# Adding expert results to the output rows in DRAM by indirect writes that add

## The chip, the cores and the metric

The kernel runs on one core of a Trainium2 chip. The metric is the device time of one execution in microseconds. A core has a matmul engine (TensorE, PE in the profile, with PEld for its weight loads), a vector engine (VectorE, DVE), an activation engine (ScalarE, ACT), a general engine (GpSimd, POOL) and a queue engine that only issues transfers here (SyncE, SP). All transfers run on 16 DMA engines. SP issues the plain ones; POOL issues the indirect ones, in which a list of row numbers in on-chip memory says which rows of a DRAM tensor are read or written, and a row number out of bounds skips its row.

## The reference, cut to what matters

The program computes two transformer blocks on 512 tokens of 1024 channels. The change touches the last stage only, the mixture of experts, which adds to each token's row the results of two experts out of 32. The two experts of a token always lie in the same group of eight.

```python
N_GROUPS = 4
EXPERTS_PER_GROUP = 8
EXPERT_FF = 256
TOP_K_EXPERTS = 2
...
    for g in range(N_GROUPS):
        a = jnp.einsum('nd,edf->nef', hf, w_gate[g])
        b = jnp.einsum('nd,edf->nef', hf, w_up[g])
        hid = jax.nn.silu(a) * b * gates[:, g, :, None].astype(hf.dtype)
        out = out + jnp.einsum('nef,efd->nd', hid, w_down[g])
    return out.reshape(B, S, D)
...
        h = rmsnorm(x, ffn_norm[l])
        x = x + hierarchical_moe(h, router_group_w[l], router_group_b[l], router_expert_w[l],
                                 router_expert_b[l], expert_w_gate[l], expert_w_up[l],
                                 expert_w_down[l])
```

`gates` is zero for the experts that a token did not choose, so the kernel computes only the chosen ones.

## The kernel before, in words

Everything up to about 1060 us is the first block, and the attention and memory attention of the second. Its last step, `cross_out` (line 1160), finishes the residual rows in an on-chip tile `fx` (4 tiles of 128 tokens by 1024 channels, 2 MB) and writes them to a DRAM tensor `x3d` (line 1175), from which the expert stage gathers rows.

**The expert stage** has 16 rounds of two experts, `2r` and `2r + 1` (line 1489). Each expert has 64 places of the 128 of a round. A list made on chip gives each place its token or none (`lists_of`, `places`); the 1024 results of 512 tokens fill about half of the 2048 places. A round:

- waits for its weights: per expert one gate and one up matrix of 1 MB each (`load_gu`, L1023 or L1026) and a down matrix of 1 MB (`load_dn`, L1039 or L1045), all issued by SP. Their buffers come from four pools of slots: `a16` has six slots of 2 MB, `w16` two, `e8` three of 1 MB, `wr` two of half a MB. `PLACES` (line 1054) says which pool the matrices of a round take, in a pattern of three rounds. In `a16`, `fx` holds one slot to the end of the program (allocated at line 1135), so five are left for gate and up matrices. The first four experts' are fetched at line 1056, the fifth's at line 1137.
- gathers its token rows from `x3d` with one indirect transfer of POOL (`fetch_rows`, L1343) into one of three tiles `hg`, three rounds ahead. Round 0 has its rows from matmuls instead (`rows_of`, L1302).
- transposes them (`turn_rows`, L1352), multiplies by gate and up (`expert_up`, L1368, `pgu`), applies the activation and the gate (L1372, L1373), transposes (L1383) and multiplies by the down matrices (`expert_down`, `pdn`).
- puts its result away in one of two manners. **Rows of a table** (10 rounds, L1392 to L1398): the two halves are copied to an on-chip tile `yr` and one indirect transfer of POOL writes its rows to a DRAM table `yd` of 1024 rows, at the token's number for its first expert and 512 further for its second. **One-hot put-back** (rounds 2, 5, 8, 11, 14 and 15, `ONEHOT` at line 1488, L1401 to L1452): the result is split into two tiles of a reduced type, a one-hot matrix is made from the token list (L1416), and 16 matmuls (L1427) with 8 additions (L1428) put the rows into `fx`. The put-back of one round is done in the next; that of round 14 is added up with that of round 15 in the same matmuls.

In the last round `results` (line 1456) reads both halves of `yd` back (L1463, 8 transfers of 512 KB), POOL adds the halves (L1464), DVE adds the sum to `fx` (L1466), and `fx` is written to `out` (L1445). `yd` is filled with zeros far earlier (line 515), in the first block.

The order of the instructions on each engine and queue is set by a scheduler that goes by its own estimate of times. It puts in the waits: an instruction waits for what it reads to be written, and a slot or a DRAM tensor is only written again when earlier uses are over.

Of the kernel before, what the change touches and what calls it, by code (L numbers as in the profile page):

```python
# [15 lines left out]
S = 512  # L16
D = 1024
# [44 lines left out]
def program(tc, I, out, sb, ps, dr, dbg, upto):  # L62
# [6 lines left out]
    def c1(shape, name, dt=F32):  # L69
        return sb.tile(shape, dt, name=name)  # L70
# [7 lines left out]
    def s4(name, shape=(128, 2, 512), dt=F32):  # L78
        return sb.tile(list(shape), dt, name=name, tag="s4", bufs=8)
# [432 lines left out]
    yd = dr.tile([2 * S, D], F32, name="yd")  # L512
    zero = s4("zero", (128, D))
    nc.gpsimd.memset(zero, 0.0)
    nc.scalar.dma_start(yd.rearrange("(i p) d -> p i d", p=128), ap_of(zero, 0, [[0, 8], [1, D]]))


# [19 lines left out]
    tk = c1([128, 8], "tk")  # L537
    nc.vector.tensor_scalar(tk[:, 0:4], ctok, -NOTOK, None, OP.add)
    nc.vector.tensor_scalar(tk[:, 4:8], ctok, S - NOTOK, None, OP.add)
# [516 lines left out]
    gus = [load_gu(e, str(e)) for e in range(4)]  # L1056
# [78 lines left out]
    fx = a16("fx", F32, (128, 4, D))  # L1135
    nc.sync.dma_start(fx, x2d.rearrange("(i p) d -> p i d", p=128))
    gus.append(load_gu(4, "4"))
# [22 lines left out]
    def cross_out(i):  # L1160
# [14 lines left out]
        nc.sync.dma_start(x3d[i * 128:(i + 1) * 128, :], xt)  # L1175

# [25 lines left out]
    def route(i):  # L1202
# [19 lines left out]
        def gates():  # L1222
# [14 lines left out]
            for j in range(2):  # L1237
                V_.tensor_scalar(R0[:, j, i, :], ohs[:, j, i, :], tk[:, 4 * j + i:4 * j + i + 1], None, OP.mult)
# [11 lines left out]
    def count(i):  # L1250

        for i2 in range(i + 1):
            nc.tensor.matmul(cnts[:, i * 32:(i + 1) * 32], trib if i2 == i else oneb, mh[:, i2, :],
                             start=i2 == 0, stop=i2 == i)
        vv = carve(2)
        V_.scalar_tensor_tensor(vv, cnts[:, i * 32:i * 32 + 2], 1.0, mh[:, i, 0:2], OP.add, OP.mult)
        V_.tensor_tensor(sel[:, i], ap_of(iota, 1, [[0, 2], [1, 64]]), ap_of(vv, 0, [[1, 2], [0, 64]]), OP.is_equal)
# [8 lines left out]
    def lists_of(p, i, src):  # L1266


        for j in range(2):
            for par in range(2):  # L1270
                nc.tensor.matmul(p[64 * par:64 * par + 64, 0:16], am[:, i, j, :],
                                 ap_of(src[:, j, i, :], par, [[2, 16]]),
                                 start=j == 0 and i == 0, stop=j == 1 and i == 3)
# [45 lines left out]
    def tokens(p, n, name):  # L1319

        src = sb.tile([128, n], I32, name=name + "_i", tag=name[:2] + "_i")
        V_.tensor_scalar(src, p, NOTOK, None, OP.add)
        e = sb.tile([128, n], F32, name=name + "_e", tag=name[:2] + "_e")
        V_.tensor_scalar(e, p, NOTOK, None, OP.add)
        return src, e

    def places(p, n):

        row, rowf = c1([128, n], "row", I32), c1([128, n], "rowf")
        V_.tensor_scalar(row, p, NOTOK, None, OP.add)  # L1330
        V_.tensor_scalar(rowf, p, NOTOK, None, OP.add)
        src, e = c1([128, n], "srci", I32), c1([128, n], "srcf")
        V_.tensor_scalar(e, rowf, float(S), -float(S), OP.is_ge, OP.mult)
        V_.tensor_tensor(e, e, rowf, OP.add)
        V_.tensor_copy(src, e)
        return row, src, e

    hg = [s4(f"hg{b}", (128, D)) for b in range(3)]
    for b in range(3):
        nc.gpsimd.memset(hg[b], 0.0)  # L1340
# [35 lines left out]
    def expert_down(sh, ws, src, name, last=False, row=None, hold=False, held=None):  # L1376

# [7 lines left out]
        if row is not None:  # L1385
            yr = s4(f"yr{name}", (128, D))
            for half in range(2):
                hs = slice(half * 512, half * 512 + 512)
                po = psm(f"pdn{name}_{half}")
                for f in range(2):  # L1390
                    for a, (gu, dn) in enumerate(ws):
                        nc.tensor.matmul(po[m * a:m * a + m, :], hd[:, f, m * a:m * a + m], dn[f][:, hs],  # L1392
                                         start=f == 0, stop=f == 1)
                if half:
                    V_.tensor_copy(yr[:, hs], po)
                else:
                    nc.scalar.activation(yr[:, hs], po, AF.Copy)
            nc.gpsimd.indirect_dma_start(out=yd, out_offset=bass.IndirectOffsetOnAxis(ap=row, axis=0), in_=yr,  # L1398
                                         in_offset=None, bounds_check=2 * S - 1, oob_is_err=False)
            return None  # L1400
        yh, yl = s4(f"yh{name}", (128, D), F32R), s4(f"yl{name}", (128, D), F32R)  # L1401
        put = []

        def down(half):
# [6 lines left out]
            split(po, yh[:, hs], yl[:, hs])  # L1411

        def where():
            put.append(w2(f"put{name}", dt=F32R))
            for i in range(4):
                V_.tensor_scalar(put[0][:, i * 128:(i + 1) * 128], iota, float(128 * i), src, OP.add, OP.is_equal)  # L1416

        def terms(i, half):
            hs = slice(half * 512, half * 512 + 512)
            return [(put[0][:, i * 128:(i + 1) * 128], t[:, hs]) for t in (yh, yl)]  # L1420

        def add(i, half):
            p = (pmm if half else psm)(f"pad{name}_{i}_{half}")
            hs = slice(half * 512, half * 512 + 512)
            ts = (held(i, half) if held else []) + terms(i, half)
            for x, (a, b) in enumerate(ts):
                nc.tensor.matmul(p, a, b, start=x == 0, stop=x == len(ts) - 1)  # L1427
            V_.tensor_tensor(fx[:, i, hs], fx[:, i, hs], p, OP.add)  # L1428

        def add_rows():  # L1430
            where()
            for i in range(4):
                for half in range(2):
                    add(i, half)

        if last:
            where()
            for half in range(2):
                down(half)
            results()  # L1440
            for half in range(2):
                hs = slice(half * 512, half * 512 + 512)
                for i in range(4):
                    add(i, half)
                    nc.sync.dma_start(out[0, i * 128:(i + 1) * 128, hs], fx[:, i, hs])  # L1445
            return None
        for half in range(2):
            down(half)
        if hold:
            where()  # L1450
            return terms
        return add_rows  # L1452

    row, srci, srcf = places(plist[:, 0:16], 16)

    def results():

        ys = [sb.tile([128, 4, D], F32, name=f"yt{j}", tag=tag, bufs=n)
              for j, (tag, n) in enumerate((("w16", 2), ("a16", 6)))]
        for i in range(4):  # L1460
            for j in range(2):
                t = ys[j][:, i, :]
                nc.sync.dma_start(t, yd[j * S + i * 128:j * S + (i + 1) * 128, :])  # L1463
            nc.gpsimd.tensor_tensor(ys[0][:, i, :], ys[0][:, i, :], ys[1][:, i, :], OP.add)  # L1464
        for i in range(4):
            V_.tensor_tensor(fx[:, i, :], fx[:, i, :], ys[0][:, i, :], OP.add)  # L1466

    for r in range(1, 4):
        fetch_rows(hg[r % 3], srci[:, r:r + 1])
# [17 lines left out]
    add_rows = None  # L1487
    ONEHOT = (2, 5, 8, 11, 14, 15)
    for r in range(16):
        es, (gtags, dtags), last = (2 * r, 2 * r + 1), PLACES[r % 3], r == 15  # L1490
        gu, fetch = [], []
        for e, tag in zip(es, gtags):
            if e < len(gus):
                gu.append(gus[e])
            else:
                t, f = load_gu(e, str(e), tag, True)
                gu.append(t)
                fetch += f
# [8 lines left out]
        rows = turn_rows(hg[r % 3], f"{r}") if r else rows0  # L1507
        sh = expert_up(rows, grs[:, 1, r:r + 1], grs[:, 0, r:r + 1], ws, f"{r}",
                       None if r else other_lists)
        if r and r + 3 < 16:  # L1510
            fetch_rows(hg[r % 3], srci[:, r + 3:r + 4])
        if add_rows and not last:
            add_rows()
        add_rows = expert_down(sh, ws, srcf[:, r:r + 1], f"{r}", last, None if r in ONEHOT else row[:, r:r + 1],
                               r == 14, add_rows if last else None)
# [6 lines left out]
    with tc.If(nval > CAP):  # L1522
        with tc.For_i(0, 32, 1) as e:
# [6 lines left out]
            for j in range(2):  # L1530
# [4 lines left out]
                V_.scalar_tensor_tensor(rx[:, :, 0], rx[:, :, 2], 0.0, tk[:, 0:4], OP.is_gt, OP.mult)  # L1535
                Rx.append(rx)
            for rr in range(4):
# [7 lines left out]
                si, sf = tokens(p[:, 0:1], 1, f"lx{rr}")  # L1545
                gx_ = sb.tile([128, 2], F32, name=f"lx{rr}_g", tag="lx_g")
                V_.tensor_copy(gx_, p[:, 1:3])
                fetch_rows(hg[rr % 3], si)
                sh = expert_up(turn_rows(hg[rr % 3], f"x{rr}"), gx_[:, 1:2], gx_[:, 0:1], ws, f"x{rr}")
                expert_down(sh, ws, sf, f"x{rr}")()  # L1550
        for i in range(4):
            nc.sync.dma_start(out[0, i * 128:(i + 1) * 128, :], fx[:, i, :])
# [21 lines left out]
```

## Time and profile before

| | |
|---|---|
| median of 3 runs | 1313.07 us (1309.04 to 1313.3) |
| the profiled execution, its own time | 1309.88 us |
| its span, from first to last instruction | 1308.1 us |
| PE busy in the span | 1263.4 us, 97% |
| DVE, ACT, POOL busy | 711.3, 490.3, 234.0 us |
| moved by the DMA engines | 218.62 MB, of which indirect 6.50 MB |
| expert stage, from the first `pgu` matmul to the end | 1059.0 to 1308.1 us |

Times in the rows are microseconds from the start of the span unless a row says ns. PE's matmuls are pipelined, and their ends are modelled, so that a busy PE is not a PE at its peak. A DMA share of 1 means that the 16 DMA engines are busy all the time. "To landing" is the time from the issue of a transfer to its completion. The idle time of an engine is put down to what released it last.

### The profile page before, as it was taken

The page shows a single profiled execution, that of the slowest core. Times are in us where ns is not written, and L with a number is a line of the kernel's source. Part 1 is how long each engine was busy: PE and PEld are TensorE (multiplying, and loading weights), DVE is VectorE, ACT ScalarE, POOL GpSimd, SP SyncE. Part 2 cuts the span into 40 slices and gives each one's busy share as a digit, 9 for nine tenths or more (in the row PEclk, how much of TensorE's full clock was granted, in tenths as well). Part 3 has the DMA queues.
Part 4 walks back from the last instruction along what each step waited for, and adds up shares of the span by engine and source line. Part 5 has one row for each costly group of instructions (what it writes and reads, how often), then busy time and mean ns, then how long its engine had stood idle before and what let it go on. Part 6 is the DMA issues. An engine that isn't in the chain of part 4 may idle for free.

```text
span 1308.1 us, 20715 instructions
## 1 busy us (share of the span) xinstructions
PE 1263.4 (97%) x8406; PEld 1000.3 (76%) x8406; DVE 711.3 (54%) x1299; ACT 490.3 (37%) x859; POOL 234.0 (18%) x278
## 2 busy tenths in 40 slices
PE   6999999999999999999999999999999999999986
PEld 5898989889988888888899977967897853343433
DVE  4567676676573244543556579993346643233225
ACT  4456454546432244422434333456435311101100
POOL 2203012030110000000001455553011120110103
PEclk9999999999999999999999999999999999999998
DMA  6321222222363243233653312224178479999995
GB/s 191 97 83 53 92 66 66 83 70 75 113 258 95 67 128 94 71 94 98 207 172 106 100 49 73 65 69 146 65 243 336 162 266 416 419 418 418 419 414 226
DMA packets 118085, 218.62 MB, mean 167 GB/s; under 512 B 15280, under 2 KB 94896, under 8 KB 106849
## 3 DMA queue, kind: packets, MB, share of 16 engines
q1 hardware_dynamic: 107248, 202.08, 42.9%
q10 hardware_dynamic: 7136, 8.67, 2.0%
q0 software_dynamic: 3600, 6.50, 1.3%
q8 instruction: 68, 1.11, 0.4%
q14 instruction: 33, 0.26, 0.1%
HBM read 206.00 MB, written 17.83 MB: 171 GB/s over the span
## 4 chain that ended last, share of the span: by engine, by line
PE 83%; DVE 6%; DMA 6%; ACT 2%; issue 1%; POOL 1%; ACTq 0%; DVEq 0%; POOLq 0%
PE pgu L1368 8%; PE pl L327 2%; PE pf L162 2%; PE pwo L161 2%; PE pf L163 2%; PE pdn L1392 2%; PE pwo L162 2%; PE pf L161 2%; PE pwo L163 2%; DMA gu<-in_expert_w_gate 2%; PE pdn L1409 1%; PE pq L163 1%; PE ps L780 1%; DMA gu<-in_expert_w_up 1%; PE pq L161 1%; PE pq L162 1%
## 5 line engine op out<-in xcount | busy, mean ns | idle before, releaser
L1368 PE MATMUL pgu<-gu,hgT 128*64 128x512 f32 x512 | 119.0, 595 | 3.7 <-DMA gu<-in_expert_w_up 2.2
L1368 PEld LDWEIGHTS pgu<-gu,hgT 128*64 128x64 f32 x512 | 39.8, 137 | 71.7 <-issue 66.4
L361 ACT ACTIVATE qk<-G 128x512 f32<-128x512 f32 x112 | 69.1, 665 | 51.6 <-DVE G L351 51.6
L1373 DVE SCALAR_TENSOR_TENSOR sh<-sh,grs,pgu 128x256 f32<-128x256 f32 x16 | 7.7, 480 | 105.4 <-ACT sh L1372 105.4
L1372 ACT ACTIVATE sh<-pgu,grs 128x256 f32<-128x256 f32 x16 | 7.6, 474 | 139.2 <-PE pgu L1368 139.2
L348 DVE TENSOR_TENSOR G<-G,T 128x512 f32<-128x512 f32 x56 | 39.2, 701 | 31.4 <-ACT qk L361 28.6
L312 POOL TENSOR_TENSOR T<-T 128x512 f32<-128x512 f32 (+6 forms) x56 | 37.0, 660 | 42.6 <-DVE T L279 38.8
L1343 POOL DMA_INDIRECT hg<-x3d,srci x15 | 15.4, 1025 | 157.5 <-PE thg L1352 109.4
L161 PE MATMUL pi<-wi,hT_h 128*128 128x256 f32 x128 | 37.8, 296 | 3.3 <-ACT wi L139 1.8
L351 DVE TENSOR_TENSOR G<-G,T 128x512 f32<-128x512 f32 x56 | 38.8, 694 | 0.0
L162 PE MATMUL pi<-wi,hT_h 128*128 128x256 f32 x128 | 37.7, 294 | 0.0
L1392 PE MATMUL pdn<-dn,sh 128*64 128x512 f32 x160 | 37.4, 601 | 0.1
L163 PE MATMUL pi<-wi,hT_l 128*128 128x256 f32 x128 | 37.3, 291 | 0.0
L161 PE MATMUL pv<-wv,hT_h 128*128 128x256 f32 x128 | 36.8, 288 | 0.0
L163 PE MATMUL pv<-wv,hT_l 128*128 128x256 f32 x128 | 36.7, 286 | 0.0
L162 PE MATMUL pv<-wv,hT_h 128*128 128x256 f32 x128 | 36.5, 286 | 0.0
L162 PE MATMUL pg<-wga,hT_h 128*128 128x256 f32 x128 | 36.5, 285 | 0.0
L161 PE MATMUL pg<-wga,hT_h 128*128 128x256 f32 x128 | 36.4, 285 | 0.0
L163 PE MATMUL pg<-wga,hT_l 128*128 128x256 f32 x128 | 36.2, 283 | 0.0
L132 POOL TENSOR_SCALAR nm_r<-nm_q 128x1 f32<-128x1 f32 x2 | 2.5, 1254 | 182.5 <-ACT nm_s L200 182.4
L327 PE MATMUL pl<-qk 128*64 128x64 f32 x896 | 34.3, 225 | 0.0
L327 PEld LDWEIGHTS pl<-qk 128*64 128x64 f32 x896 | 29.3, 137 | 6.2 <-issue 2.1
(554 smaller groups left out, 4080.9 us busy)
## 6 DMA issues: line engine op xcount, KB each, us to landing
gu<-in_expert_w_gate SPq DMA_DIRECT2D x32, 1024.0 KB, 19.3
gu<-in_expert_w_up SPq DMA_DIRECT2D x32, 1024.0 KB, 18.4
dn<-in_expert_w_down SPq DMA_DIRECT2D x27, 1024.0 KB, 20.0
wo_r<-in_w_out SPq DMA_DIRECT2D x16, 512.0 KB, 3.6
wq_r<-in_w_in SPq DMA_DIRECT2D x12, 512.0 KB, 4.3
dn<-in_expert_w_down SPq DMA_DIRECT2D x10, 512.0 KB, 18.1
wi_r<-in_w_in SPq DMA_DIRECT2D x8, 512.0 KB, 6.5
wfb_r<-in_w_in SPq DMA_DIRECT2D x8, 512.0 KB, 4.3
```

The source lines that it names most:

```text
L161: nc.tensor.matmul(o, ah, bh, start=first, stop=False)
L162: nc.tensor.matmul(o, ah, bl, start=False, stop=False)
L163: nc.tensor.matmul(o, al, bh, start=False, stop=last)
L312: nc.gpsimd.tensor_tensor(ap_of(T, o, [[n2, 2], [1, n2]]), ap_of(T, a, [[sa, 2], [2, n2]]), ap_of(T, a + 1, [[sa, 2], [2, n2]]), OP.mult)
L327: nc.tensor.matmul(p[64 * j:64 * j + 64, c * 64:c * 64 + 64], kt[:, k0:k0 + 64], qt[:, q0:q0 + 64], start=True, stop=True)
L348: nc.vector.tensor_tensor(ap_of(G, 0, [[512, 2], [2 * m, nb], [1, m]]), ap_of(G, 0, [[512, 2], [2 * m, nb], [1, m]]), ap_of(T, a + 1, [[sa ...
L351: nc.vector.tensor_tensor(ap_of(G, 1024 + m, [[512, 2], [2 * m, nb], [1, m]]), ap_of(G, 1024 + m, [[512, 2], [2 * m, nb], [1, m]]), ap_of( ...
L361: nc.scalar.activation(ap_of(qk, a * 512, [[2 * m, nb], [m, 2], [1, m]]), ap_of(G, a * 512, [[2 * m, nb], [1024 + m, 2], [1, m]]), AF.Copy)
L780: nc.tensor.matmul(p[:, :n], qiT[hs, h // 2, i * 128:(i + 1) * 128], kiT[hs, :n], start=True, stop=True)
L1343: nc.gpsimd.indirect_dma_start(out=h, out_offset=None, in_=x3d, in_offset=bass.IndirectOffsetOnAxis(ap=sidx, axis=0), bounds_check=S - 1, ...
L1368: nc.tensor.matmul(pg[m * a:m * a + m, :], hT_[:, k, m * a:m * a + m], ap_of(gu, k * 256, [[2048, 2], [1, 256]]), start=k == 0, stop=k == 7)
L1392: nc.tensor.matmul(po[m * a:m * a + m, :], hd[:, f, m * a:m * a + m], dn[f][:, hs], start=f == 0, stop=f == 1)
```

## The change

`yd`, its zeros and the one-hot put-back go. `cross_out` writes each finished tile of residual rows to `out` as well as to `x3d`. Every round's result rows are copied to an on-chip tile and added to the rows of `out` by one indirect write of POOL that adds (`compute_op=OP.add`). [...] There are four tiles `hg` instead of three, and a round's result takes the tile from which its own token rows came, so the gather for round `r + 4` follows the write of round `r` on POOL and in the tile. `fx` is allocated ahead of the weights and has its last use before the expert rounds. The lists hold token numbers alone, without the offset of 512 for second experts. The loop for lists of more than 64 tokens (line 1522 on, not entered in the profiled execution) is changed to match.

```diff
-    yd = dr.tile([2 * S, D], F32, name="yd")
-    zero = s4("zero", (128, D))
-    nc.gpsimd.memset(zero, 0.0)
-    nc.scalar.dma_start(yd.rearrange("(i p) d -> p i d", p=128), ap_of(zero, 0, [[0, 8], [1, D]]))
...
-    gus = [load_gu(e, str(e)) for e in range(4)]
+    fx = a16("fx", F32, (128, 4, D))
+    gus = [load_gu(e, str(x)) for x, e in enumerate((0, 16, 1, 17))]
...
-    fx = a16("fx", F32, (128, 4, D))
     nc.sync.dma_start(fx, x2d.rearrange("(i p) d -> p i d", p=128))
-    gus.append(load_gu(4, "4"))
+    gus.append(load_gu(2, "4"))
...
         nc.sync.dma_start(x3d[i * 128:(i + 1) * 128, :], xt)
+        nc.sync.dma_start(out[0, i * 128:(i + 1) * 128, :], xt)
...
-    hg = [s4(f"hg{b}", (128, D)) for b in range(3)]
-    for b in range(3):
+    hg = [s4(f"hg{b}", (128, D)) for b in range(4)]
+    for b in range(4):
         nc.gpsimd.memset(hg[b], 0.0)
...
-    def expert_down(sh, ws, src, name, last=False, row=None, hold=False, held=None):
+    def expert_down(sh, ws, src, yr, name):
...
+        for half in range(2):
             hs = slice(half * 512, half * 512 + 512)
             po = psm(f"pdn{name}_{half}")
             for f in range(2):
                 for a, (gu, dn) in enumerate(ws):
                     nc.tensor.matmul(po[m * a:m * a + m, :], hd[:, f, m * a:m * a + m], dn[f][:, hs],
                                      start=f == 0, stop=f == 1)
-            split(po, yh[:, hs], yl[:, hs])
...
+            if half:
+                V_.tensor_copy(yr[:, hs], po)
+            else:
+                nc.scalar.activation(yr[:, hs], po, AF.Copy)
+        nc.gpsimd.indirect_dma_start(out=out[0], out_offset=bass.IndirectOffsetOnAxis(ap=src, axis=0), in_=yr,
+                                     in_offset=None, bounds_check=S - 1, oob_is_err=False, compute_op=OP.add)
...
-    ONEHOT = (2, 5, 8, 11, 14, 15)
     for r in range(16):
-        es, (gtags, dtags), last = (2 * r, 2 * r + 1), PLACES[r % 3], r == 15
+        es, (gtags, dtags) = (r, r + 16), PLACES[r % 3]
...
-        if r and r + 3 < 16:
-            fetch_rows(hg[r % 3], srci[:, r + 3:r + 4])
-        if add_rows and not last:
-            add_rows()
-        add_rows = expert_down(sh, ws, srcf[:, r:r + 1], f"{r}", last, None if r in ONEHOT else row[:, r:r + 1],
-                               r == 14, add_rows if last else None)
+        expert_down(sh, ws, srci[:, r:r + 1], hg[r % 4], f"{r}")
+        if r + 4 < 16:
+            fetch_rows(hg[r % 4], srci[:, r + 4:r + 5])
```

## Rows read from the trace of the kernel before

**Rows 1.** One stretch: length, busy PE, PEld, DVE, ACT, POOL, clock, DMA share, GB/s.

```profile
1080.00:1280.00 200.00, 184.58 (x853) 77.07 (x851) 61.44 (x117) 23.34 (x47) 20.17 (x20) 1.00 1.01 417
```

**Rows 2.** PE's own waits from 1060 us: total us, times, longest.

```profile
PE pgu L1368 <- DMA gu<-in_expert_w_up: 2.2, 2, 1.1
```

**Rows 3.** The chain that ended last: start, us, what.

```profile
1261.31 18.08 DMA gu<-in_expert_w_up
...
1279.53 3.62 PE pgu L1368 x14
```

**Rows 4.** The chain, rounds 0 and 1 and, three on, 4: the activation's start.

```profile
1067.26 0.48 ACT sh L1372
...
1080.72 0.48 ACT sh L1372
...
1123.40 0.48 ACT sh L1372
```

**Rows 5.** POOL, a gather and the table write after it: start, us, idle before.

```profile
1143.46 0.98 POOL L1343 DMA_INDIRECT hg<-x3d,srci  x1 [12.44 <-PE thg L1352]
1144.74 1.04 POOL L1398 DMA_INDIRECT yd<-yr,row  x1 [0.30 <-issue]
```

**Rows 6.** SP's queue, four weight transfers in a row: start, us.

```profile
1147.56 0.33 SPq L1039 DMA_DIRECT2D dn<-in_expert_w_down  x1
1150.71 0.33 SPq L1045 DMA_DIRECT2D dn<-in_expert_w_down  x1
1153.82 0.33 SPq L1039 DMA_DIRECT2D dn<-in_expert_w_down  x1
1156.33 0.33 SPq L1026 DMA_DIRECT2D gu<-in_expert_w_gate  x1
```

**Rows 7.** A stretch that holds the zero fill of yd (columns of Rows 1).

```profile
360.00:380.00 20.00, 20.00 (x131) 17.95 (x131) 19.34 (x29) 7.39 (x10) 5.35 (x4) 1.00 0.79 313
```

**Rows 8.** Stretches of 5 us ahead of the second round (columns of Rows 1).

```profile
1055.00:1060.00 5.00, 5.00 (x84) 4.27 (x86) 3.05 (x14) 0.56 (x1) 0.00 (x0) 1.00 0.02 5
1060.00:1065.00 5.00, 5.00 (x24) 1.42 (x18) 0.00 (x0) 0.72 (x1) 3.29 (x3) 1.00 0.82 295
1065.00:1070.00 5.00, 3.89 (x21) 1.74 (x22) 1.52 (x4) 0.86 (x2) 0.00 (x0) 1.00 0.77 264
```

**Rows 9.** The last matmuls that read fx, and the next gate matrix on SP.

```profile
1056.26 2.05 PE L1302 MATMUL rows<-sel,fx 128*128 128x128 f32 x16
...
1066.41 0.33 SPq L1026 DMA_DIRECT2D gu<-in_expert_w_gate  x1
```

**Rows 10.** Rounds 13 and 14 in order of time: down product, table write, up, down.

```profile
1257.52 3.65 PE L1392 MATMUL pdn<-dn,sh 128*64 128x512 f32 x16
...
1262.66 0.97 POOL L1398 DMA_INDIRECT yd<-yr,row  x1 [11.32 <-DMA dn<-in_expert_w_down]
...
1263.92 7.05 PE L1368 MATMUL pgu<-gu,hgT 128*64 128x512 f32 x30 [1.11 <-DMA gu<-in_expert_w_up]
...
1273.10 3.65 PE L1409 MATMUL pdn<-dn,sh 128*64 128x512 f32 x16
```

**Rows 11.** Gathers (tile hg): issue to landing.

```profile
DMA to landing us min/median/max: 4.4/8.3/9.5
```

**Rows 12.** Table writes (tile yr): the group with first and last start; issue to landing.

```profile
L1398 POOL DMA_INDIRECT yd<-yr,row x10: 973/1014/1042, 1075.1 to 1262.7; - x10
...
DMA to landing us min/median/max: 7.9/9.8/10.9
```

**Rows 13.** The last two writes of the output, and the landing time of such a write.

```profile
1302.90 0.93 SPq L1445 DMA_DIRECT2D out<-fx  x2
...
out<-fx SPq DMA_DIRECT2D x8, 256.0 KB, 2.4
```

**Rows 14.** POOL, a table write that waits for the one before it.

```profile
1241.68 1.00 POOL L1398 DMA_INDIRECT yd<-yr,row  x1 [9.88 <-DVE fx L1428]
1250.37 0.97 POOL L1398 DMA_INDIRECT yd<-yr,row  x1 [7.68 <-DMA yd<-yr,row]
```

More of the change, by code (lines that the diff above doesn't have):

```diff
@@ L536, in program @@
     nc.gpsimd.memset(oneb, 1.0)
-    tk = c1([128, 8], "tk")
-    nc.vector.tensor_scalar(tk[:, 0:4], ctok, -NOTOK, None, OP.add)
-    nc.vector.tensor_scalar(tk[:, 4:8], ctok, S - NOTOK, None, OP.add)
+    tk = c1([128, 4], "tk")
+    nc.vector.tensor_scalar(tk, ctok, -NOTOK, None, OP.add)
     kvm = e8("kvm", (128, 2, 1024))
@@ L1237, in gates @@
             for j in range(2):
-                V_.tensor_scalar(R0[:, j, i, :], ohs[:, j, i, :], tk[:, 4 * j + i:4 * j + i + 1], None, OP.mult)
+                V_.tensor_scalar(R0[:, j, i, :], ohs[:, j, i, :], tk[:, i:i + 1], None, OP.mult)
             r = rs[:, i:i + 1]
@@ L1255, in count @@
         vv = carve(2)
-        V_.scalar_tensor_tensor(vv, cnts[:, i * 32:i * 32 + 2], 1.0, mh[:, i, 0:2], OP.add, OP.mult)
+        V_.scalar_tensor_tensor(vv, ap_of(cnts, i * 32, [[16, 2]]), 1.0, ap_of(mh, i * 32, [[16, 2]]), OP.add, OP.mult)
         V_.tensor_tensor(sel[:, i], ap_of(iota, 1, [[0, 2], [1, 64]]), ap_of(vv, 0, [[1, 2], [0, 64]]), OP.is_equal)
@@ L1271, in lists_of @@
                 nc.tensor.matmul(p[64 * par:64 * par + 64, 0:16], am[:, i, j, :],
-                                 ap_of(src[:, j, i, :], par, [[2, 16]]),
+                                 ap_of(src[:, j, i, :], 16 * par, [[1, 16]]),
                                  start=j == 0 and i == 0, stop=j == 1 and i == 3)
@@ L1322, in tokens @@
         V_.tensor_scalar(src, p, NOTOK, None, OP.add)
[L1323 to L1336, printed above, removed]
-    hg = [s4(f"hg{b}", (128, D)) for b in range(3)]
-    for b in range(3):
+        return src
+    hg = [s4(f"hg{b}", (128, D)) for b in range(4)]
+    for b in range(4):
         nc.gpsimd.memset(hg[b], 0.0)
@@ L1384, in expert_down @@
         nc.scalar.activation(hd, tp[:, :256].rearrange("p (f t) -> p f t", f=2), AF.Copy)
[L1385 to L1404, printed above, removed]
+        for half in range(2):
             hs = slice(half * 512, half * 512 + 512)
@@ L1410, in down @@
                                      start=f == 0, stop=f == 1)
-            split(po, yh[:, hs], yl[:, hs])
[L1413 to L1466, printed above, removed]
+            if half:
+                V_.tensor_copy(yr[:, hs], po)
+            else:
+                nc.scalar.activation(yr[:, hs], po, AF.Copy)
@@ L1468, in program @@
+        nc.gpsimd.indirect_dma_start(out=out[0], out_offset=bass.IndirectOffsetOnAxis(ap=src, axis=0), in_=yr,
+                                     in_offset=None, bounds_check=S - 1, oob_is_err=False, compute_op=OP.add)
+    srci = tokens(plist[:, 0:16], 16, "lists")
     for r in range(1, 4):
-        fetch_rows(hg[r % 3], srci[:, r:r + 1])
+        fetch_rows(hg[r % 4], srci[:, r:r + 1])
     grs = c1([128, 2, 16], "grs")
@@ L1485, in other_lists @@
         V_.tensor_copy(nmi, nmx)
-    add_rows = None
-    ONEHOT = (2, 5, 8, 11, 14, 15)
     for r in range(16):
-        es, (gtags, dtags), last = (2 * r, 2 * r + 1), PLACES[r % 3], r == 15
+        es, (gtags, dtags) = (r, r + 16), PLACES[r % 3]
         gu, fetch = [], []
-        for e, tag in zip(es, gtags):
-            if e < len(gus):
-                gu.append(gus[e])
+        for x, (e, tag) in enumerate(zip(es, gtags)):
+            if 2 * r + x < len(gus):
+                gu.append(gus[2 * r + x])
             else:
-                t, f = load_gu(e, str(e), tag, True)
+                t, f = load_gu(e, f"{r}_{x}", tag, True)
                 gu.append(t)
@@ L1506, in program @@
         ws = list(zip(gu, dn))
-        rows = turn_rows(hg[r % 3], f"{r}") if r else rows0
+        rows = turn_rows(hg[r % 4], f"{r}") if r else rows0
         sh = expert_up(rows, grs[:, 1, r:r + 1], grs[:, 0, r:r + 1], ws, f"{r}",
                        None if r else other_lists)
-        if r and r + 3 < 16:
-            fetch_rows(hg[r % 3], srci[:, r + 3:r + 4])
-        if add_rows and not last:
-            add_rows()
-        add_rows = expert_down(sh, ws, srcf[:, r:r + 1], f"{r}", last, None if r in ONEHOT else row[:, r:r + 1],
-                               r == 14, add_rows if last else None)
+        expert_down(sh, ws, srci[:, r:r + 1], hg[r % 4], f"{r}")
+        if r + 4 < 16:
+            fetch_rows(hg[r % 4], srci[:, r + 4:r + 5])
     nval = nc.values_load(nmi[0:1, 0:1], min_val=0, max_val=S)
@@ L1534, in program @@
                     V_.tensor_reduce(rx[:, :, 1 + c], t, AX.X, OP.add)
-                V_.scalar_tensor_tensor(rx[:, :, 0], rx[:, :, 2], 0.0, tk[:, 0:4], OP.is_gt, OP.mult)
+                V_.scalar_tensor_tensor(rx[:, :, 0], rx[:, :, 2], 0.0, tk, OP.is_gt, OP.mult)
                 Rx.append(rx)
@@ L1544, in program @@
                                          start=j == 0 and i == 0, stop=j == 1 and i == 3)
-                si, sf = tokens(p[:, 0:1], 1, f"lx{rr}")
+                si = tokens(p[:, 0:1], 1, f"lx{rr}")
                 gx_ = sb.tile([128, 2], F32, name=f"lx{rr}_g", tag="lx_g")
                 V_.tensor_copy(gx_, p[:, 1:3])
[L1548 to L1552, printed above, removed]
+                fetch_rows(hg[rr], si)
+                sh = expert_up(turn_rows(hg[rr], f"x{rr}"), gx_[:, 1:2], gx_[:, 0:1], ws, f"x{rr}")
+                expert_down(sh, ws, si, hg[rr], f"x{rr}")
 def kernel(**inputs):
```

## The prediction

> **What bounds the kernel now.** I read the stretches of the expert stage first. From 1080 to 1280 us the 16 DMA engines are busy all the time, at 417 GB/s, while PE is busy for 184.6 of 200 us [rows 1]. So the stage has two limits close together, and the waits tell which ends last. PE waits for weights only twice, 1.1 us each time [rows 2], in the last two rounds. That looks as if PE were the limit, but the chain that ended last shows the other one: it goes back through the last up matrix, issued at 1261.3 and awaited until 1279.5 [rows 3]. PE ran through a lead of prefetched weights in the earlier rounds and has used it up at the end. A round without put-back takes PE 13.46 us, three rounds with one put-back 42.68, 14.2 each [rows 4]. The DMA engines need more. Where SP is held back only by the transfers ahead, it issues a 1 MB weight transfer every 2.51 us, and after the gather at 1143.5 and the table write at 1144.7 [rows 5] two steps took 3.15 and 3.11 [rows 6]. An indirect transfer thus costs the engines about 0.62 us, in either direction. Three rounds are 18 MB of weights, three gathers and two table writes: 18 x 2.51 + 5 x 0.62 = 48.3 us, 16.1 a round. **The time of the last up matrix, call it U, is set by the DMA engines**, and the end is U plus a tail of 1308.1 - 1279.5 = 28.6 us.
>
> **What costs or brings nothing.** The put-backs of rounds 2, 5, 8 and 11 leave PE's path ahead of U, each worth 42.68 - 3 x 13.46 = 2.3 us there [rows 4], 9 us in all. This shows nowhere, since PE then only waits longer for weights: 13.46 against 16.1 us a round. The weights' transfers are the cover; were they early, the 9 us would be gained. The zero fill (4 MB, in the stretch from 360) ran while PE was busy for 20 of 20 us [rows 7]: nothing. The four new writes of residual rows are 512 KB each, 1.25 us of DMA time by the weight rate, while the engines are nearly idle: 0.02 busy from 1055 to 1060 [rows 8]. SP waits for the same row tile at the write to `x3d` just before, so no new wait either. The one memset more and the list arithmetic less lie on POOL and DVE beside PE's row matmuls: nothing.
>
> **The head start.** `fx` is free when its last matmuls end, at 1058.3, so gate and up of one more expert can be asked for then. Before, the next gate matrix waited for round 0 to release its slot and was issued at 1066.4 [rows 9]. These two transfers are 5 us of DMA time, but the engines have only 2.05 us idle between 1060 and 1070 (shares 0.82 and 0.77), and about one more just before 1060 [rows 8]. I take 2.5 us off U; bounds 0 (the scheduler uses the slot otherwise) and 5. Taking `fx` ahead of the weights also delays the fourth expert's matrices until an older tile of the attention goes, well ahead of round 1 where they are read: nothing; a late one would show as a wait of PE there.
>
> **More and dearer writes ahead of U.** Rounds 2, 5, 8 and 11 now write as well: 4 x 0.62 = 2.5 us. And 14 writes (rounds 0 to 13) now add. No row shows a write that adds. It must read its 64 or so destination rows from DRAM as a gather does and write them as a table write does. Below, the read lies beside the write at no cost; above, it costs what a gather costs, 0.62 us. That it might be quicker than a plain write is excluded by the same bytes still being written. I take the upper value, since the nearest row to the added part is a gather, which slowed the weights by a full share. 14 x 0.62 = 8.7 us, against 0. [...] No row here shows which.
>
> **The tail.** In round 14 the awaited matmuls start at 1263.9 and the down product at 1273.1, 9.2 us later; in round 13 the write was issued 5.1 us after the down product's start [rows 10]. So the last write is issued at U + 14.3. Its landing at an idle queue lies between the lightest gather, 4.4 us [rows 11], and the slowest table write under load, 10.9 [rows 12]. I take 5.9: the light gather plus the 1.5 us by which the median write exceeds the median gather (9.8 against 8.3), near the low end because the weights are in by then. From the landing of the last output write to the end of the span were 1308.1 - (1303.5 + 2.4) = 2.2 us [rows 13]. Tail 14.3 + 5.9 + 2.2 = 22.4 against 28.6: **6.2 us less** (bounds 7.7 and 1.2). The table's reading, POOL's and DVE's additions, the last put-back and eight output writes are all in that difference.
>
> **The queue of POOL.** A new wait: the gather of round r + 4 overwrites the tile that write r is reading, so it waits for that write to land, and the next write, behind it in POOL's queue and on the same rows of `out`, waits too. Table writes already wait for each other: one issued at 1241.7 landed after 7.9 us, the least of all [rows 12], and the next, held back by it, followed at 1250.4, 0.8 us later [rows 14]. A cycle is then landing + 0.8 + 1.3 (gather to write [rows 5]) while gathers are left, landing + 0.8 after. Gathers have a lead of three rounds, so PE does not notice; the last write does, if a cycle is longer than a round. Landing lies between 9.8, a table write, and 18.1, a gather and a table write one after the other [rows 11, 12]. I take 12, nearer to the write, since issuing and queueing are paid once: cycle 14.1, below the 16 us of a round at DMA pace.
>
> **The sum.** U: -2.5 + 2.5 + 8.7 = +8.7. Tail: -6.2. Together +2.5 us. The profiled execution took 1309.9 us by its own time (span 1308.1), 3.2 below the median of 1313.1; it would become 1312.4, and the median 1315.6.
>
> **The cases.** A measurement of this kernel tells about 0.3%, 3.9 us, from no change.
>
> - **A, reads are full price (forecast, 0.40):** +2.5, median 1315.6; with its bounds 1311 to 1321.
> - **B, the added read is hidden (0.33):** U stays, the tail brings 6.2 us: 1306.9. [...] Against it: gathers and table writes cost the same, so whatever they load is not one side's port. With the larger head start and the quickest landing it is 1303.
> - **C, the writes wait for each other (0.27):** the last write is due at 1279.5 + 8.7 + 14.3 = 1302.5, the first was issued at 1075.1 before [rows 12], so 15 cycles must fit into 227 us. 12 cycles carry a gather: 15 x landing + 12 x 2.1 + 3 x 0.8 = 227 gives 13.3 us (12.7 if the reads are hidden). From there each microsecond of landing costs 15. At 14 us the last write goes out at 1312.7 and the span ends at 1320.8: 12.7 us slower, median 1325.8. At 18 it would be over 70. For it: loaded writes take up to 10.9 without reading; against it: 13.3 is well above that. [...]
>
> From these: faster by over 0.3% 0.31 (nearly all of B), within 0.3% 0.33 (most of A, a little of B and C), slower 0.36 (the rest of A, most of C). The range is 1303, the low end of B, to 1334, which is C at a landing of about 14.5; beyond lies the rest of C.
>
> **What would show it.** Steps of SP's issues under load of 3.7 us or more per adding write mean A, 3.1 B. U near 1288 and a last write some 14 us behind it: A; U near 1280: B. POOL idle before a gather on its own write for more than 13 us, and the last write long after the last down product: C. One more gate and up pair issued at about 1058 shows the head start. Wrong altogether if PE no longer waits for weights in the last rounds, or if DMA share falls below 1 between 1080 and 1270.

## The result and the profile after

The changed kernel takes 1319.18 us (median of 5 runs, 1317.18 to 1319.33), the kernel before beside it on the same chip 1310.73 (5 runs, 1308.56 to 1313.3): a ratio of 1.0055, 95% interval 1.0042 to 1.0068. It is slower by 8.45 us, where 2.5 were forecast. The time itself is 3.6 us above the forecast's 1315.6, and would be 5.9 above it on the median that the forecast stood on, 1313.07, which was 2.3 us higher than this one. The profiled spans show the same, 1316.8 against 1308.1, +8.7 us.

The long stretch of the expert stage, in the columns of [rows 1]:

```profile
1080.00:1280.00 200.00, 169.90 (x752) 70.45 (x750) 31.32 (x52) 18.89 (x39) 33.03 (x25) 0.98 1.02 399
```

The DMA engines are as busy as before (share 1.02 against 1.01) and move less, 399 GB/s against 417. PE is busy for 14.7 us less in this stretch: the put-backs are gone, and it is further behind and waits (752 matmuls instead of 853, of which the four put-backs were 64). Its waits for weights, and what POOL waits for, by the view of waits from 1060 us (total us, times, longest), beside [rows 2]:

```profile
POOL hg L1324 <- DMA out<-hg,lists_i: 63.9, 7, 9.4
...
PE pgu L1349 <- DMA gu<-in_expert_w_up: 4.8, 3, 2.7
```

The end of the timeline of PE, in the manner of [rows 3, 10], with start, us and idle time before:

```profile
1290.03 1.07 PE L1349 MATMUL pgu<-gu,hgT 128*64 128x512 f32 x2
1291.75 7.05 PE L1349 MATMUL pgu<-gu,hgT 128*64 128x512 f32 x30 [0.64 <-DMA gu<-in_expert_w_up]
1299.93 0.51 PE L1363 MATMUL thd<-csq,sh 128*128 128x128 f32 x2 [1.13 <-DVE sh L1354]
1300.91 3.65 PE L1370 MATMUL pdn<-dn,sh 128*64 128x512 f32 x16 [0.47 <-ACT sh L1364]
```

and that of POOL, whose last instruction with work this is:

```profile
1290.95 1.55 POOL L1376 DMA_INDIRECT out<-hg,lists_i  x1 [15.15 <-DVE hgT L1342]
1306.06 1.55 POOL L1376 DMA_INDIRECT out<-hg,lists_i  x1 [13.55 <-DVEq L1430]
```

So U, the start of the last matmuls that wait for an up matrix, is 1291.75 against 1279.53: **+12.2 us**. What is behind U takes 1316.8 - 1291.75 = 25.05 us against 28.6: **-3.5 us**. These two make the 8.7. The stage itself begins 0.7 us later in this profile (first `pgu` matmul at 1059.68 against 1058.96), which is part of the 12.2. The adding writes as a group, by the view of the tile `out` (duration in ns, first and last start; then issue to landing, to compare with [rows 12]):

```profile
L1376 POOL DMA_INDIRECT out<-hg,lists_i x16: 1552/1587/1609, 1075.3 to 1306.1; - x16
...
DMA to landing us min/median/max: 6.3/9.9/11.2
```

Part 3 of the page gives packets, MB and the time of the packets as a share of 16 engines' span. The indirect transfers are the `software_dynamic` ones; before, they were

```profile
q0 software_dynamic: 3600, 6.50, 1.3%
```

and after

```profile
q0 software_dynamic: 4464, 8.10, 2.5%
```

A quarter more bytes (8.10 MB for 6.50) take nearly twice the time (2.5% for 1.3%).

The head start, to compare with [rows 9, 8]: SP's queue, where the pair of the next expert now stands ahead of 1060,

```profile
1059.09 0.33 SPq L1019 DMA_DIRECT2D gu<-in_expert_w_gate  x1
1059.48 0.43 SPq L1019 DMA_DIRECT2D gu<-in_expert_w_up  x1
1060.08 0.33 SPq L1038 DMA_DIRECT2D dn<-in_expert_w_down  x1
1067.13 0.33 SPq L1019 DMA_DIRECT2D gu<-in_expert_w_gate  x1
```

and the stretches of 5 us, whose DMA share (last but one) is now full between 1060 and 1070:

```profile
1060.00:1065.00 5.00, 5.00 (x25) 1.71 (x22) 0.06 (x1) 1.28 (x1) 3.29 (x3) 1.00 0.99 360
1065.00:1070.00 5.00, 3.44 (x17) 0.96 (x13) 0.82 (x3) 0.86 (x2) 0.00 (x0) 1.00 1.02 411
```

### The profile page after: what moved, and what is told of

It is laid out like the page before. It is cut to its first block, busy times and chain, and to the rows that moved or that the text cites. A ratio compares the mean times of both kernels' runs of the same rounds, so it can differ in the third digit from the quotient of the medians.

```text
span 1316.8 us, 20434 instructions
## 1 busy us (share of the span) xinstructions
PE 1249.6 (95%) x8310; PEld 991.9 (75%) x8310; DVE 670.8 (51%) x1220; ACT 486.4 (37%) x853; POOL 238.7 (18%) x280
## 5 line engine op out<-in xcount | busy, mean ns | idle before, releaser
L1349 PE MATMUL pgu<-gu,hgT 128*64 128x512 f32 x512 | 123.0, 608 | 8.9 <-DMA gu<-in_expert_w_up 4.8
L1349 PEld LDWEIGHTS pgu<-gu,hgT 128*64 128x64 f32 x512 | 47.1, 139 | 72.5 <-issue 63.6
L1370 PE MATMUL pdn<-dn,sh 128*64 128x512 f32 x256 | 62.1, 599 | 8.5 <-ACT sh L1364 6.2
L1353 ACT ACTIVATE sh<-pgu,grs 128x256 f32<-128x256 f32 x16 | 7.6, 473 | 161.9 <-PE pgu L1349 161.9
L348 DVE TENSOR_TENSOR G<-G,T 128x512 f32<-128x512 f32 x56 | 39.3, 701 | 31.4 <-ACT qk L361 28.6
L1373 DVE COPY hg<-pdn 128x512 f32<-128x512 f32 x16 | 11.1, 692 | 76.7 <-PE pdn L1370 76.7
L1370 PEld LDWEIGHTS pdn<-dn,sh 128*64 128x64 f32 x256 | 17.9, 136 | 41.7 <-issue 27.0
L1376 POOL DMA_INDIRECT out<-hg,lists_i x16 | 25.3, 1582 | 97.3 <-issue 54.6
L1324 POOL DMA_INDIRECT hg<-x3d,lists_i x15 | 15.7, 1048 | 119.9 <-DMA out<-hg,lists_i 63.9
```

Source lines behind the costliest of these rows:

```text
L348: nc.vector.tensor_tensor(ap_of(G, 0, [[512, 2], [2 * m, nb], [1, m]]), ap_of(G, 0, [[512, 2], [2 * m, nb], [1, m]]), ap_of(T, a + 1, [[sa ...
L1324: nc.gpsimd.indirect_dma_start(out=h, out_offset=None, in_=x3d, in_offset=bass.IndirectOffsetOnAxis(ap=sidx, axis=0), bounds_check=S - 1, ...
L1349: nc.tensor.matmul(pg[m * a:m * a + m, :], hT_[:, k, m * a:m * a + m], ap_of(gu, k * 256, [[2048, 2], [1, 256]]), start=k == 0, stop=k == 7)
L1376: nc.gpsimd.indirect_dma_start(out=out[0], out_offset=bass.IndirectOffsetOnAxis(ap=src, axis=0), in_=yr, in_offset=None, bounds_check=S - ...
```

## The experiments

The theory after the result: the addition of an adding write is paid in full by the DMA engines that also bring the weights, and U is late by that. Two sizes were off: U rose by 3.5 us more than the sum said, and the tail fell by 2.7 us less. For the first the suspicion was that the engines are loaded unevenly, for the second that the program's end after an indirect transfer is longer. Rivals: the addition is hidden, the writes wait for each other (case C), or the new wait of the gathers delays something.

**The same write without the addition.**

```diff
-    in_offset=None, bounds_check=S - 1, oob_is_err=False, compute_op=OP.add)
+    in_offset=None, bounds_check=S - 1, oob_is_err=False)
```

> The kernel after, with indirect writes that overwrite rows of the output instead of adding to them: the addition is left out, so the output holds one result a row; lists, order and waits are the same. U is the time at which PE goes on with the last awaited up matrix (1279.5 us before, 1291.7 after). Theory 1, the added read costs the DMA engines as much as a gather: 14 writes ahead of U save 14 x 0.62 = 8.7 us on the mean engine and somewhat more on the busiest one, U 1280 to 1283, time 0.990 to 0.994 of after, so 0.996 to 1.000 of before; 4096-byte packets of the indirect writes take about 160 ns as in the kernel before. Theory 2, the writes cost what waits cost (each waits for the one before, gathers wait for writes): the waits are all still there, U moves by less than 2 us, 1.004 to 1.007 of before. Theory 3, uneven load of the DMA engines is the main part: U falls by half of it, about 6 us, since every row then weighs half.

Measured: 1304.16 us, ratio to the kernel before 0.9945 (0.9926 to 0.9963), span 1302.5. The timelines of PE and POOL at the end, the view of the tile `out`, and part 3 of the page:

```profile
1280.18 7.37 PE L1349 MATMUL pgu<-gu,hgT 128*64 128x512 f32 x32
```

```profile
1294.82 0.97 POOL L1376 DMA_INDIRECT out<-hg,lists_i  x1 [12.73 <-DVEq L1430]
```

```profile
L1376 POOL DMA_INDIRECT out<-hg,lists_i x16: 973/1007/1013, 1075.8 to 1294.8; - x16
...
DMA to landing us min/median/max: 3.2/8.0/9.0
```

```profile
q0 software_dynamic: 4464, 8.09, 1.6%
```

The addition alone costs 14.3 us of the spans (1316.8 - 1302.5); the ratio lies below the 0.996 to 1.000 that was expected, and is far from the 1.004 to 1.007 of the theory of waits. The 32 matmuls of the last round run through without a wait for weights; the last such wait is 1.42 us in the round before. The packets' time falls from 2.5% of 1316.8 us to 1.6% of 1302.5 at the same number of packets. Summed from the records of single packets behind these shares it is 11.8 us of all 16 engines for 16 writes, 0.73 us each. The records say why: an indirect packet of 4096 bytes has a median of 159 ns in the kernel before and here, and 327 over all of the changed kernel's, in which the adding ones are the slow half (944 of 1973 took 150 to 170 ns, 989 took 320 to 330). Issue on POOL (0.97 against 1.55 us) and landing at the end (3.2 against 6.3) are shorter too, 3.1 us of the tail.

**The places of an expert spread over the partitions.** An expert has 64 places, and its tokens, 17 to 51 and 32 on average, filled the first of them. The edit puts neighbouring positions four places apart, so that any number of tokens is spread over all groups of four partitions. The same rows go to the same experts.

```diff
+    SPREAD, PLACE = [[64, 2], [4, 8], [1, 4]], [[0, 2], [1, 8], [8, 4]]
...
-        V_.tensor_tensor(sel[:, i], ap_of(iota, 1, [[0, 2], [1, 64]]), ap_of(vv, 0, [[1, 2], [0, 64]]), OP.is_equal)
+        for h in range(2):
+            V_.tensor_tensor(ap_of(sel, i * 128 + 32 * h, SPREAD), ap_of(iota, 1 + 32 * h, PLACE),
+                             ap_of(vv, 0, [[1, 2], [0, 8], [0, 4]]), OP.is_equal)
```

(and the same for `am`, with `ap_of(iota, 32 * h, PLACE)` and `ap_of(pos, i * 2, ...)`). It was made in the changed kernel and in the kernel before.

> The kernel after, with the places of an expert's list spread over its 64 partitions in steps of four (place 8l + e of each half goes to partition 4e + l) instead of filled from partition 0; the output is the same. In the kernel after the weight packets of the last transfers end up to 12 us apart from engine to engine (13.5 busy at 1283, 4 at 1290, none at 1297). Theory 3, rows in the first partitions fall to the same few DMA engines, in groups of four neighbouring partitions to an engine: the spread evens this out, the engines end within 5 us of each other, U falls by 5 to 9 us, 0.998 to 1.002 of before. Theory 3b, rows fall to the engines in turn (partition modulo 16): then this order makes it worse, U rises by 3 to 6 us, 1.008 to 1.011. Theory 1 alone, only the sum of the reads counts: U within 1.5 us, 1.004 to 1.007.

> The kernel before, with the places spread over the partitions in the same way; the output is the same. Theory 3: 22 indirect transfers ahead of U, all plain, weigh about 14 engine-packets a row pair less than the adding ones, so U falls by 2 to 5 us, 0.996 to 0.9985 of before. Theory 3b: U rises by 1 to 3 us, 1.001 to 1.002. Theory 1 alone: the same within 0.15%.

Measured: the changed kernel with it 1310.8 us, ratio to the kernel before 0.9992 (0.9983 to 1.0002); the kernel before with it 1307.52, 0.9973 (0.9962 to 0.9984). The last awaited matmuls in the timeline of PE of the changed kernel,

```profile
1284.64 7.05 PE L1355 MATMUL pgu<-gu,hgT 128*64 128x512 f32 x30 [0.15 <-DMA gu<-in_expert_w_up]
```

and of the kernel before:

```profile
1276.23 3.62 PE L1374 MATMUL pgu<-gu,hgT 128*64 128x512 f32 x14 [1.01 <-DMA gu<-in_expert_w_up]
```

U falls by 7.1 us in the one and by 3.3 in the other. In the changed kernel the last write also lands sooner, 5.0 us after its issue instead of 6.3, and the two make the 8.4 us of the spans. At even load the change raises U by 1284.64 - 1276.23 = 8.4 us, where the sum had 8.7; the other 3.8 us of the 12.2 go when the load is evened. The kernel before with spread places is the fastest here that leaves nothing out: 4.0 us less than the kernel before beside it (1311.48).

**The opposite order.** If the place decides which engine moves a row, an order that fills few groups of four must cost.

```diff
-    SPREAD, PLACE = [[64, 2], [4, 8], [1, 4]], [[0, 2], [1, 8], [8, 4]]
+    SPREAD, PLACE = [[64, 2], [4, 8], [1, 4]], [[0, 2], [8, 8], [1, 4]]
...
-        ap_of(iota, 1 + 32 * h, PLACE)
+        ap_of(iota, 1 + 4 * h, PLACE)
```

> The changed kernel, with the places of an expert's tokens put so that neighbouring positions share a group of four partitions: positions 0 to 7 go to places 0 to 3 and 32 to 35, 8 to 15 to places 4 to 7 and 36 to 39, and so on. The number of rows and bytes, the lists and the waits stay. [...] Rival (places do not matter to the engines, and the gain of the spread order came from the lists or from chance): U within 2 us of 1291.75, ratio 1.003 to 1.008.

Measured: 1337.86 us, ratio to the kernel before 1.0198 (1.0179 to 1.0217). The long stretch, PE's waits, and the last awaited matmuls:

```profile
1080.00:1280.00 200.00, 167.66 (x702) 66.65 (x700) 28.98 (x48) 17.44 (x36) 31.47 (x24) 0.94 0.99 371
```

```profile
PE pdn L1376 <- DMA dn<-in_expert_w_down: 12.0, 9, 2.5
...
PE pgu L1355 <- DMA gu<-in_expert_w_up: 3.0, 5, 1.0
```

```profile
1310.74 7.05 PE L1355 MATMUL pgu<-gu,hgT 128*64 128x512 f32 x30 [0.60 <-DMA gu<-in_expert_w_up]
```

With the same packets and bytes U is 19.0 us later, and 371 GB/s come instead of 399. The last 6 us ahead of U in the changed kernel, with spread places, and in this order show it most directly (the DMA share is the last but one):

```profile
1285.75:1291.75 6.00, 5.33 (x24) 1.86 (x23) 2.02 (x3) 0.60 (x2) 0.80 (x1) 1.00 0.30 126
```

```profile
1278.64:1284.64 6.00, 5.82 (x27) 2.14 (x26) 2.02 (x3) 0.98 (x2) 0.30 (x1) 1.00 0.85 357
```

```profile
1304.74:1310.74 6.00, 5.38 (x23) 1.88 (x23) 2.02 (x3) 0.65 (x2) 0.75 (x1) 1.00 0.37 158
```

Ahead of U the engines' share is 0.30 in the changed kernel and 0.37 in this order, while PE waits for a matrix, and 0.85 with spread places. The mean load ahead of U does not tell the three apart: 15 gathers and 14 writes at 159 ns a gathered and 327 ns an added row are 27.9 us over 16 engines (an estimate) in each, and U is 1284.64 with spread places, 1291.75 in the changed kernel and 1310.74 in this order. Within one kernel U thus follows how the rows are placed, 7.1 us down and 19.0 up, and not that mean. The rival of the expectation, U within 2 us of 1291.75 and a ratio of 1.003 to 1.008, falls.

**Both edits: plain writes and spread places.**

> The kernel after with both edits: places spread over the partitions, and indirect writes that overwrite instead of adding (the addition is left out). At an even load the price of adding stands alone: spread alone was 0.9992 of before, overwriting alone 0.9945. Theory 1, 14 added reads of 0.62 us ahead of U and 3 us less for the landing of the last write (3.2 us overwriting, 6.3 adding, in the two profiles): 8 to 12 us below spread alone, 0.990 to 0.993, or a little less if PE becomes the limit in the last rounds, since U cannot show below the end of PE's own work. Rival, the price of adding was mostly the busiest engines' (both edits cure the same thing): 0.994 to 0.996.

Measured: 1299.24 us, ratio 0.9907 (0.9892 to 0.9922). The end of PE's and POOL's timelines:

```profile
1263.05 7.05 PE L1355 MATMUL pgu<-gu,hgT 128*64 128x512 f32 x30 [1.06 <-DMA gu<-in_expert_w_up]
...
1276.43 7.25 PE L1355 MATMUL pgu<-gu,hgT 128*64 128x512 f32 x32
```

```profile
1290.95 0.98 POOL L1382 DMA_INDIRECT out<-hg,lists_i  x1 [12.60 <-DVEq L1436]
```

The two costs are two: evening the load still brings 4 to 5 us when no write adds (spans 1302.5 - 1298.5, medians 1304.16 - 1299.24), and the addition still costs 10 to 12 us when the load is even (spans 1308.4 - 1298.5, medians 1310.8 - 1299.24; the runs of each pair were made on different chips). The last wait for weights is now in round 14, so PE takes over as the limit at the end, and the price of the addition at even load is at least this.

**The head start undone.** DVE reads `fx` in round 15, so that its slot stays taken as before.

```diff
+        if name == "15":
+            V_.tensor_tensor(c1([128, 1], "hold"), yr[:, 0:1], fx[:, 0, 0:1], OP.add)
```

> The kernel after, but one element of fx is read once more by DVE in the last round, so that fx keeps its slot to the end as before and five slots are left for gate and up matrices: the head start undone alone. Theory of the prediction, head start 2.5 us off U: U rises by 2 to 3 us, 1.007 to 1.008 of before. Rival, the head start was used up by a later wait for a slot or by the engines' uneven load: U within 1 us, 1.005 to 1.006. Rival, one slot more is worth both transfers: 5 us, 1.009.

Measured: 1322.58 us, ratio to the kernel before 1.0085 (1.0068 to 1.0103), where the changed kernel had 1.0055. SP's next gate matrix and PE's last awaited matmuls:

```profile
1067.68 0.33 SPq L1019 DMA_DIRECT2D gu<-in_expert_w_gate  x1
```

```profile
1294.44 7.05 PE L1349 MATMUL pgu<-gu,hgT 128*64 128x512 f32 x30 [2.93 <-DMA gu<-in_expert_w_up]
```

U is 2.7 us later, the median 3.4. The head start is worth about that.

**The result in a tile of its own.** The gather no longer waits for the write whose tile it fills.

```diff
+        yr = s4(f"yr{name}", (128, D))
         for half in range(2):
```

> The kernel after, but each round's result goes to a tile of its own instead of the tile of its token rows, so that the gather four rounds on need not wait for the write to land; writes still wait for each other. Theory: this wait is free, 1.004 to 1.007 of before, U within 1 us of 1291.7. Rival (the queue of POOL is part of the loss): 1.000 to 1.003. A second rival: gathers go out earlier and crowd the first rounds' weights, up to 1.008.

Measured: 1318.55 us, ratio 1.0053 (1.0039 to 1.0067), as the changed kernel. POOL's waits (total us, times, longest):

```profile
POOL hg L1324 <- DVE yr L1374: 101.8, 8, 16.6
POOL out L1377 <- DMA out<-yr,lists_i: 36.6, 4, 9.9
```

The gather's wait for the write is gone, the writes now wait for one another where the gather had waited ahead of them, and the time stays. The wait cost nothing that shows. The profiled execution is the slowest of the five (1321.12 us); its last gate and up matmuls start at 1294.27, 2.5 us later than in the changed kernel, and it settles nothing finer than the median does.

**The last round written by SP**, plainly, to a DRAM tensor that is no longer read.

```diff
+        if name == "15":
+            nc.sync.dma_start(x3d[0:128, :], yr)
+            return
```

> The kernel after, but the last round's rows are written in one plain block by SP to a scratch tensor instead of being added to the output (the additions of round 15 are left out). In the kernel after, 4.4 us pass from the landing of the last write to the end of the span, against 2.2 before. Theory, POOL needs the time to close after its last indirect transfer: with that transfer one round earlier it is hidden, and 2.0 to 2.5 us pass from the landing of SP's write to the end; the span is 1309.5 to 1311.5. Rival, the end is longer whatever writes last: 4 us or more still, span 1312 to 1314.

Measured: 1312.81 us (one run), span 1310.9 against 1316.8. The write's issue on SP, and its landing by part 6 of the page (KB each, us to landing):

```profile
1305.69 0.33 SPq L1377 DMA_DIRECT2D x3d<-hg  x1
```

```profile
x3d<-hg SPq DMA_DIRECT2D x1, 512.0 KB, 3.8
```

The issue is 0.4 us earlier than POOL's of 1306.06, the landing 2.5 us shorter (3.8 against 6.3), and from landing to the end are 1310.9 - (1305.69 + 3.8) = 1.4 us (2.0 to 2.5 were expected) instead of 1316.8 - (1306.06 + 6.3) = 4.4. The three make the 5.9 us of the spans. What fills most of the 4.4 stands in the raw record of the changed kernel, after the landing (start, us):

```
1312.56   0.81 GpSimd INC_SWDGE_SEM
1313.40   2.60 GpSimd DRAIN
```

The closing instructions of all other engines follow this drain, from 1316.17 us on. In this experiment POOL's last indirect write was issued at 1292.04 and landed 6.0 us later; the two steps, if as long, are over at about 1301.5 (an estimate), well before SP's write lands at 1309.5.

## Why the prediction was right and wrong

**The mechanism was that of case A.** U is set by the DMA engines, the addition is paid in full (0.73 us of the engines a write, where the forecast had 0.62 for the added read), and PE's relief shows nowhere. Case B, the hidden read at 1306.9, falls: an adding packet takes twice the time of a plain one (327 against 159 ns), and without the addition the kernel is 14 us faster (spans of 1302.5 against 1316.8). That the added time is a read was an assumption; no view shows one. The forecast's price was about right too: 14 x 0.62 = 8.7, less 2.5 for the head start and 2.5 more for four writes, made +8.7 for U; at even load U rose by 8.4. That this meets the 8.7 so closely is in part luck: with the packets' own 0.73 us a write and the head start of 2.7 the same sum gives 14 x 0.73 + 2.5 - 2.7 = 10.0. The four writes were not tried alone, so how the 8.4 divide stays open within some 2 us.

**PE's relief was not there to be covered.** The forecast took 9 us off PE's own path and said that only the late weights hid them. But rounds 0 to 8, before the weights are late, take 113.25 us in the changed kernel (the activation L1353 starts at 1067.97 and 1181.22) and 112.27 before. From round 4 on a round takes PE 14.35 us, not 13.46: the transposes of the next rows now stand in one piece behind the down product, where before half of them filled the pause ahead of it. PE waits for its neighbours instead, 10.3 us in all,

```profile
PE pdn L1370 <- ACT sh L1364: 6.2, 13, 0.5
PE pgu L1349 <- DVE hgT L1342: 4.1, 12, 0.4
```

which is about what the put-backs had cost. Early weights would not have brought the 9 us: with plain writes and spread places, rounds still take 14.35. U did not feel this, as the DMA engines set it.

**Two smaller readings of the forecast.** The four writes of residual rows go out from 1014.1 to 1044.5 us, not in the idle stretch from 1055 that the forecast priced them by; from 1040 to 1055 the engines are now full (1.01 against 0.80), and they are free again behind it (0.08). What they cost can at most be the 0.7 us by which the stage begins later. And the bounds of case A, added up, reach 1323, not 1321: without a head start and with a tail only 1.2 shorter it is 2.5 + 2.5 + 5.0 = 10.0 us.

**Where the signs were looked for.** "Steps of 3.7 us" of SP do not stand alone. Behind the gather of 1155.62 and the write of 1159.46 SP's steps are 2.49, 3.15, 3.36 and 2.72 us: the excess over 2.51 is spread over four transfers, 1.7 us in all against the 1.9 (0.62 + 1.24) of the sum.

**The step that failed for U** is "an indirect transfer thus costs the engines about 0.62 us". That is a mean over 16 engines, but PE waits until a matrix is complete, and in the last 6 us ahead of U only 0.30 of the engines were still at work. The 0.62 was read from rounds of the kernel before, whose own unevenness (3.3 us of U, from the run with spread places) it did not show as such. In the changed kernel the same order of places costs 7.1, where the write of a lopsided list comes in every round and each of its rows takes 327 ns instead of 159 (that the rounds also pair other experts, `r` and `r + 16`, was not tried alone). The difference, 3.8 us, is what U rose above the 8.4. The same skew is in the stretches of 5 us ahead of U in the changed kernel, whose DMA share (last but one) falls long before U while the awaited matrix is on the way:

```profile
1280.00:1285.00 5.00, 3.87 (x17) 1.31 (x14) 0.48 (x1) 0.47 (x1) 0.00 (x0) 1.00 0.92 323
1285.00:1290.00 5.00, 4.97 (x26) 2.22 (x26) 1.19 (x2) 0.98 (x2) 0.00 (x0) 1.00 0.36 152
```

The trace does not record which engine moved a packet. The runs bear out Theory 3 against Theory 3b by U alone: 7.1 us down with the places spread in steps of four, where 3b had 3 to 6 up, and 19.0 up with the groups of four filled one after another.

**The tail.** Its first term was exact: the last write is issued at U + 14.3, as forecast. The landing was 6.3 us for 5.9. The term that failed is "from the landing to the end of the span were 2.2 us": it was carried over from a plain write of SP [rows 13] to an indirect one of POOL, and measured 4.4. So the tail gave back 3.5 us instead of 6.2.

**Case C did not decide.** POOL's timeline shows the chain that it spoke of, gather after write:

```profile
1145.11 1.59 POOL L1376 DMA_INDIRECT out<-hg,lists_i  x1 [2.60 <-issue]
1155.62 1.03 POOL L1324 DMA_INDIRECT hg<-x3d,lists_i  x1 [8.93 <-DMA out<-hg,lists_i]
1159.46 1.59 POOL L1376 DMA_INDIRECT out<-hg,lists_i  x1 [2.80 <-issue]
1170.23 1.03 POOL L1324 DMA_INDIRECT hg<-x3d,lists_i  x1 [9.18 <-DMA out<-hg,lists_i]
```

A cycle is 14.35 us, where the forecast had 14.1, but it is not this chain's. It is PE's round: the write of 1159.46 waits for the second half of its own product, which DVE finishes at 1158.66:

```profile
1157.97 0.69 DVE L1373 COPY hg<-pdn 128x512 f32<-128x512 f32 x1 [4.76 <-PE pdn L1370]
```

All 16 writes go out 0.75 to 0.85 us after that copy, so none is held by the write before it. The chain alone would take 10.5 us from the write to the gather that waits for its landing, where 12.8 were taken, and 1.0 for the gather's issue; it had 2 us to spare here and 0.8 at the least (round 2). The landing was 9.9 us in the median and 11.2 at most, under the 13.3 from which it would have set the time. With tiles of their own the time is the same.

**The sum** was thus +8.7 - 6.2 = +2.5 and came out as +12.2 - 3.5 = +8.7: 3.8 us for uneven engines less 0.3 for the rest of U, 2.2 for the end, 0.4 for the landing. It stayed inside the bounds of case A, on the side of "slower by over 0.3%", to which the text had given "the rest of A".

## What to carry to other kernels

Price an indirect write that adds as it measured here, about a write and a gather of the same rows (327 ns a packet against 159, and 0.73 us of the engines a write for the addition), and charge it to whatever the DMA engines are bringing at that time; here they had no room, and U rose by more than the shorter tail gave back. A last transfer that goes by POOL also lengthened the program's end, by 3 us against one of SP (4.4 against 1.4 from its landing). Where a list of rows is shorter than its places, spread the valid rows over the partitions: it brought 8 us here in the changed kernel and 4 in the one before, and in the changed kernel the engines' share in the last 6 us ahead of U was 0.85 with it and 0.30 without. Before a mean price per transfer is multiplied, look whether the DMA share falls well ahead of the last awaited landing, for then it is not the mean that ends last. The sign shows only where nothing is queued behind the weights: in the kernel before, with the reading of `yd` behind them, the share stayed at 1.00 in the 6 us ahead of U, and only the run with spread places showed its 3.3 us.

## What the runs showed that was not expected

- The order of an expert's places, with the same rows and bytes, moves the time from 0.9992 to 1.0198 of the kernel before.
- An indirect packet of 4096 bytes that adds takes 327 ns against 159, the issue on POOL 1.55 us against 0.97, and the last landing 6.3 us against 3.2 (5.0 with spread places).
- After POOL's last indirect transfer had landed its closing took another 0.81 and 2.60 us in the changed kernel. From that landing to the end were 4.4 us there and 1302.5 - (1294.82 + 3.2) = 4.5 without the addition, against 1.4 after SP's write.
